# The first stage of a hybrid encoder layer: three row tiles with the contraction outside, shared modulation rows, and TensorE kept busy in waits

## The chip, the cores and the metric

The kernel runs on one core of one Trainium2 chip. A core has five engines, each with a queue of its own that runs in order: TensorE (PE, matmuls; its weight loads are PEld), VectorE (DVE), ScalarE (ACT), GpSimd (POOL) and SyncE (SP, which issues most transfers here). The metric is the time of one execution on the device in microseconds (us); lower is better.

## The reference

One layer of an encoder over x of 2048 rows and 1024 channels, in f32. What matters here is its beginning:

```
mod = silu(c) @ w_mod + b_mod                       # 6 x 1024 values
shift1, scale1, ... = split(mod, 6)
hmix = rms_norm(x, g_norm1) * (1.0 + scale1) + shift1
proj = hmix @ w_in                                  # 1024 x 2832
q_a, k_a, v_a, q_m, k_m, v_m, o_m, gates = split(proj)
```

Behind it come windowed attention and a chunked mLSTM in both directions, an output projection, and a SwiGLU feed-forward part, each with its modulation, and a last norm. These are not touched.

## The kernel before

The rows are worked in tiles of 128 (`tt`, 0 to 15), four of which make a block `n` (512 rows). The channels are worked in tiles of 128 as well (`k`, 0 to 7, `KT` = 8); `z` = 0 is the half with k from 0 to 3, `z` = 1 the half from 4 to 7. Products keep f32 accuracy by splitting each operand in a high and a low part; `mm3` (L56 to L58) issues three matmuls for one product: high by high, high by low, low by high.

The first stage makes, for every row tile, the columns of the projection that are needed in row order: 128 for the attention's values and 16 gates (with 128 of the mLSTM's values they make the 272 columns of `pa`), and the other 384 of the mLSTM's values (`pv`). `nat_mm` (L397) runs over k for `pa` and then for `pv`. The weights come in raw (`wnr`, `load_nat`, L330) and `split_nat` (L340) makes the high part `wnh` on ScalarE and the low part `wnl` on VectorE and GpSimd in turns (L342 to L347).

The moving-in of a block of x: `squares` (L163) sums the squares of its four row tiles on ScalarE (L168), `rsqrt` (L92) takes the root on VectorE in twelve small instructions, `scaled` (L171) multiplies (block 0 on ScalarE, L175; the others on VectorE, L177). `turned` (L179) turns one channel tile of the block by four transposes on TensorE (L183), and ScalarE applies scale and shift while reading it out of PSUM (`ntmp`, L184). `turned_split` (L186) splits the outcome in the high and low part of `hT` on VectorE (L190, L191). The scale `gs1` is (1 + scale1) x g_norm1.

Scale and shift are the modulation rows m = 1 and m = 0. Each half row (m, z) takes 1024 x 512 weights, loaded by `load_mod` (L195, four loads of 512 KB, L201) into eight slots, of which (1, 0) and (1, 1) share four and (0, 0) and (0, 1) the other four. `mod_sum` (L206) works one half row: VectorE multiplies the weights of a channel tile by its value of silu(c) and adds them up in `macc` (L213 the first, L215 the others). For (1, 0) and (0, 1) TensorE does the first four of the eight channel tiles instead (L220: one column of silu(c) against 512 columns of weights, in f32, so two records each) and adds the sum over the partitions of `macc` to them (L221); ScalarE copies the row (L223) and TensorE lays it out as four columns (L226). For the other two, TensorE lays out `macc` directly (L230). `mod_bias` (L237) adds b_mod on VectorE, `scales` (L328) makes gs1.

The order of this stage is written out by hand (L404 to L439). TensorE keeps the order of the program in the whole kernel. The other engines keep it up to `pre.close()` (L439); instructions from behind that line are put between those of the hand-ordered part by a scheduler that works from estimated times. The order on TensorE is: m = 1's and m = 0's columns for z = 0, the turns of channel tiles 0 to 3 of block 0, the projection of row tiles 0, 1 and 2 one after the other over k = 0 to 3, then the modulation for z = 1, the turns of channel tiles 4 to 7, and then the loop over n and i (L444), which finishes row tiles 0, 1 and 2 over k = 4 to 7 and goes on with row tile 3 and the other blocks. In it `EVERY` says after how many steps of `nat_mm` a channel tile of the next block is turned. A row tile's columns are read out of PSUM by ScalarE and VectorE (L478 to L482) and stored.

SP's queue loads, in this order: c, x of block 0, the weights of (1, 0) and (0, 0), the first half of `wnr`, (1, 1), the second half of `wnr`, (0, 1), x of blocks 1 and 2 (each tile 512 KB, L293), and the small rows. `columns_of` (L308) turns small rows (biases, gains, convolution weights) into columns; the second such turn (L452) stands ahead of row tile 4.

PSUM has eight banks, handed out by `bank` (L52) under the letters g, a, c (two each) and b, d (one each). A bank or an SBUF slot is handed on only when its last reader is done.

## Time and profile before

| | |
|---|---|
| median of 3 runs | 2271.92 us (2271.91 to 2275.42) |
| the profiled execution | 2273.35 us |
| its span, first to last instruction | 2271.6 us |
| mean granted TensorE clock | 0.996 |

A row of a timeline gives the start in us from the span's start, the duration, the engine, the line and the operation, out<-in by the program's names, their sizes, how many instructions are merged in the row, and in brackets how long the engine had been idle before it and what released it. A row of the windows gives a stretch of time, its length, the busy time of PE, PEld, DVE, ACT and POOL with the number of instructions that start in it, then the granted TensorE clock, the busy share of the DMA engines and their GB/s.

### The profile page before, as it was taken

Reading aid. Unit: us, or ns where it says so; the run is one execution under the profiler, and the core shown is the slowest. Engines: PE = TensorE matmul, PEld = TensorE weight load, DVE = VectorE, ACT = ScalarE, POOL = GpSimd, SP = SyncE. Lnnn points to the kernel's source line nnn. Section 1 sums busy time; section 2 is a strip of 40 time slices with the busy share of each in tenths; the row PEclk is TensorE's granted clock in tenths of the full one; section 3 lists DMA queues with packets and bytes.
Section 4 is the critical chain, followed back from the end, with each engine's and each line's share of the span. In section 5 each row is a group of like instructions: output and inputs, shape, how many; then the busy total and the mean of one; then the engine's idle time right before and its main releaser. Section 6 shows DMA issues by size and latency. Waiting matters only on the chain.

```text
span 2271.6 us, 32440 instructions
## 1 busy us (share of the span) xinstructions
PE 2222.6 (98%) x10822; PEld 1856.6 (82%) x10822; DVE 1618.5 (71%) x2931; ACT 1059.6 (47%) x2206; POOL 1065.6 (47%) x927
## 2 busy tenths in 40 slices
PE   6999999999999999999999999999999999999998
PEld 4997888888888878788888888788888888888886
DVE  6787577656788887786767786766767666785594
ACT  4533656544687746354445444433333333233352
POOL 1006635434334334536666665657565654692020
PEclk9999999999999999999999999999999999999999
DMA  8577755675766576764343454433333374542462
GB/s 321 171 245 220 236 168 168 186 239 173 214 186 180 172 244 209 258 239 152 109 145 114 149 181 162 158 98 111 98 112 98 112 251 148 168 152 94 142 219 93
DMA packets 352811, 391.28 MB, mean 172 GB/s; under 512 B 21260, under 2 KB 251004, under 8 KB 352644
## 3 DMA queue, kind: packets, MB, share of 16 engines
q1 hardware_dynamic: 352420, 389.18, 52.3%
q8 instruction: 85, 1.39, 0.3%
q14 instruction: 82, 0.67, 0.1%
q10 hardware_dynamic: 224, 0.04, 0.0%
HBM read 269.95 MB, written 119.19 MB: 171 GB/s over the span
## 4 chain that ended last, share of the span: by engine, by line
PE 55%; DMA 1%; DVE 1%; issue 1%; POOL 1%; ACT 0%; SPq 0%; POOLq 0%; ACTq 0%
PE fp L56 12%; PE fp L57 12%; PE fp L58 12%; PE fo L57 6%; PE fo L58 6%; PE fo L56 6%; PE ops L56 1%; PE ops L57 1%; PE ops L58 1%; DMA al<-a_d 0%; PE trn L183 0%; DMA T<-hop_d 0%; DMA a_d<-c 0%; DVE T L1417 0%; DMA w2n<-in_w_ffn_out_dram 0%
## 5 line engine op out<-in xcount | busy, mean ns | idle before, releaser
L498 PE MATMUL gps<-hT,whi 128*128 128x512 f32 x1088 | 395.4, 418 | 0.3 <-DVE cacc L513 0.3
L57 PE MATMUL fo<-w,ah 128*128 128x512 f32 x616 | 239.8, 389 | 0.7 <-DVE w L1726 0.7
L58 PE MATMUL fo<-w,al 128*128 128x512 f32 x616 | 239.9, 389 | 0.0
L56 PE MATMUL fo<-w,ah 128*128 128x512 f32 x616 | 239.7, 389 | 0.0
L498 PE MATMUL gps<-hT,wlo 128*128 128x512 f32 x544 | 226.0, 416 | 0.0
L498 PEld LDWEIGHTS gps<-hT,whi 128*128 128x128 f32 x1088 | 199.4, 190 | 24.3 <-DVE cacc L513 0.7
L56 PE MATMUL fp<-T,S 128*128 128x512 f32 x528 | 206.7, 391 | 0.2 <-ACT s L1613 0.2
L57 PE MATMUL fp<-T,S 128*128 128x512 f32 x528 | 205.7, 389 | 0.0
L58 PE MATMUL fp<-T,S 128*128 128x512 f32 x528 | 205.4, 389 | 0.0
L1717 DVE TENSOR_TENSOR al<-al,ah 128x1024 fp32r<-128x1024 f32 x77 | 116.4, 1516 | 107.7 <-ACT ah L1716 107.6
L1716 ACT ACTIVATE ah<-al 128x1024 fp32r<-128x1024 f32 x77 | 81.5, 1060 | 183.1 <-DMA al<-a_d 180.3
L1456 DVE TENSOR_TENSOR S<-sf,S 128x512 fp32r<-128x512 f32 x86 | 132.4, 1577 | 34.3 <-ACT S L1455 34.1
L1621 DVE SCALAR_TENSOR_TENSOR g<-t,g 128x512 f32<-128x512 f32 x44 | 46.4, 1055 | 131.8 <-ACT t L1620 131.8
L1456 DVE TENSOR_TENSOR A<-graw,A 128x512 fp32r<-128x512 f32 x86 | 132.1, 1556 | 11.5 <-ACT A L1455 11.5
L58 PE MATMUL fp<-B,A 128*128 128x512 f32 x352 | 136.9, 389 | 0.0
L56 PE MATMUL fp<-B,A 128*128 128x512 f32 x352 | 136.9, 389 | 0.0
L57 PE MATMUL fp<-B,A 128*128 128x512 f32 x352 | 136.9, 389 | 0.0
L57 PEld LDWEIGHTS fo<-w,ah 128*128 128x128 f32 x616 | 115.6, 188 | 25.1 <-DVE w L1726 1.1
L58 PEld LDWEIGHTS fo<-w,al 128*128 128x128 f32 x616 | 115.6, 188 | 24.5 <-DVE al L1717 0.3
L56 PEld LDWEIGHTS fo<-w,ah 128*128 128x128 f32 x616 | 115.6, 188 | 24.1
L798 POOL TENSOR_SCALAR ap<-ap,adn 128x384 f32<-128x384 f32 (+1 forms) x128 | 72.0, 582 | 126.7 <-PE atp L805 61.9
L1460 POOL TENSOR_TENSOR sf<-A,A22r 128x512 f32<-128x512 f32 x43 | 59.6, 1387 | 147.0 <-DMA A22r<-in_w_ffn_in_dram 131.9
(418 smaller groups left out, 6166.5 us busy)
## 6 DMA issues: line engine op xcount, KB each, us to landing
al<-a_d SPq DMA_DIRECT2D x77, 512.0 KB, 4.0
wmod<-in_w_mod_dram SPq DMA_DIRECT2D x48, 512.0 KB, 7.3
graw<-in_w_ffn_in_dram SPq DMA_DIRECT2D x43, 512.0 KB, 3.6
a_d<-ka SPq DMA_DIRECT2D x66, 256.0 KB, 4.6
bc<-bc_d SPq DMA_DIRECT2D x64, 256.0 KB, 3.7
hop_d<-n SPq DMA_DIRECT2D x56, 256.0 KB, 4.4
a_d<-u SPq DMA_DIRECT2D x55, 256.0 KB, 4.4
mqk<-qk_d SPq DMA_DIRECT2D x44, 256.0 KB, 3.9
```

The costliest lines, as they stand in the source:

```text
L56: pe.matmul(o, lh, rh, start=first, stop=False, skip_group_check=skip)
L57: pe.matmul(o, lh, rl, start=False, stop=False, skip_group_check=skip)
L58: pe.matmul(o, ll, rh, start=False, stop=last, skip_group_check=skip)
L498: pe.matmul(ps, w[i == 2][:, k, :], hT[n](i == 1, k), start=(k == 0 and i == 0), stop=(k == KT - 1 and i == 2))
L798: pool.tensor_scalar(self.p[g][:, :self.NK], self.p[g][:, :self.NK], dn[:, g:g + 1], 0.0, MUL, ADD)
L1456: dve.tensor_tensor(t[:, 1, :], f, t[:, 0, :].bitcast(F32), SUB)
L1460: pool.tensor_tensor(f1, a21, a22, ADD)
L1621: dve.scalar_tensor_tensor(g0, t0, 1.0, g0, ADD, MUL)
L1716: act.activation(ah, al.bitcast(F32), AF.Copy)
L1717: dve.tensor_tensor(al, al.bitcast(F32), ah.bitcast(F32), SUB)
```

## The change

Five things are changed, all in the first stage. (1) Row tiles 0, 1 and 2 are worked together, with k outside (`three`): as soon as a channel tile is split, the three row tiles use it. Channel tiles 0 to 2 are used before the second half's modulation, 3 in the middle of it, 4 to 6 behind it, and 7 in the loop. The weights' high and low parts are made one channel tile ahead (`nat_hi`, `nat_lo`), all low parts on VectorE. (2) The modulation's half rows become objects (`Mod`). TensorE's and VectorE's shares are interleaved; (0, 0) has two of its eight channel tiles on TensorE, (1, 1) none, the other two four. Row and sums of (0, 0) and (0, 1) are added as columns in PSUM, not as a row. The weights of (0, 1) are loaded ahead of the second half of `wnr`. (3) VectorE's sums of (1, 1) and (0, 1) follow each other without a break. (4) `steady` issues f32 matmuls of x by the identity into a bank that nobody reads, nine in all. (5) The second turn of small rows moves from ahead of row tile 4 to behind row tile 5. Besides, `scaled` gives two of the four row tiles of every block to ScalarE.

```diff
@@ -171,70 +171,83 @@
     def scaled(xt, r, on_act=False):
 
         for i in range(4):
-            if on_act:
+            if on_act or i % 2:
                 act.activation(xt[i], xt[i], AF.Copy, scale=r[:, i:i + 1])
             else:
                 dve.tensor_scalar(xt[i], xt[i], r[:, i:i + 1], None, MUL)
 
-    def turned(t, xt, k, tag, gs, shift):
...
+    def turns(xt, k, tag):
 
         ps = bank(tag, "trn")
         for i in range(4):
             pe.transpose(ps[:, i * P:(i + 1) * P], xt[i][:, k * P:(k + 1) * P], ident)
+        return ps
+
+    def turned(t, xt, k, tag, gs, shift):
+
+        act.activation(t, turns(xt, k, tag), AF.Identity, bias=shift[:, k:k + 1], scale=gs[:, k:k + 1])
+
+    def turned_split(pl, xt, k, gs, shift, dst, ps=None):
+
+        t = pl.tile([P, 512], F32, tag="ntmp", name="ntmp", bufs=2)
+        if ps is None:
+            ps = turns(xt, k, "bd"[k % 2])
         act.activation(t, ps, AF.Identity, bias=shift[:, k:k + 1], scale=gs[:, k:k + 1])
...
+    class Mod:
+
+
+        def __init__(self, m, z):
+            self.m, self.z, self.acc, self.ps, self.w = m, z, None, None, []
+            for k in range(0, KT, 2):
+                w = big(wm_slots[0], "wmod", (P, 2, 512), F32)
+                wm_slots.rotate(-1)
+                sp.dma_start(w, w_mod[k * P:(k + 2) * P, m * D + z * 512:m * D + (z + 1) * 512]
+                             .rearrange("(k p) c -> p k c", p=P))
+                self.w.append(w)
+
+        def sums(self, pl, ks):
+
+            for k in ks:
+                w = self.w[k // 2][:, k % 2, :]
+                if self.acc is None:
+                    self.acc = pl.tile([P, 512], F32, tag="macc", name="macc")
+                    dve.tensor_scalar(self.acc, w, sc_col[:, k:k + 1], None, MUL)
+                else:
+                    dve.scalar_tensor_tensor(self.acc, w, sc_col[:, k:k + 1], self.acc, MUL, ADD)
+
+        def rows(self, ks, tag, joined):
+
+            self.ps = bank(tag, "modrow")
+            for k in ks:
+                pe.matmul(self.ps[:1, :], sc_col[:, k:k + 1], self.w[k // 2][:, k % 2, :], start=k == ks[0],
+                          stop=k == ks[-1] and not joined)
+
+        def join(self):
+            pe.matmul(self.ps[:1, :], ones[:, 0:1], self.acc, start=False, stop=True)
+
+        def copy(self, pl):
+            self.row = pl.tile([1, 512], F32, tag="mrow", name="mrow", bufs=1)
+            act.activation(self.row, self.ps[:1, :], AF.Copy)
+
+        def columns(self, ps, row, first, last):
+
+            self.cs = ps
+            src, one = (self.row, ones[:1, 0:1]) if row else (self.acc, ones[:, 0:1])
             for k in range(4):
-                pe.matmul(ps[:, k:k + 1], row[:, k * P:(k + 1) * P], ones[:1, 0:1], start=True, stop=True)
-        else:
-            ps = bank("d", "modps")
-            for k in range(4):
-                pe.matmul(ps[:, k:k + 1], acc[:, k * P:(k + 1) * P], ones[:, 0:1], start=True, stop=True)
-        yield True
-        mod_bias(m, z, ps)
-        yield True
-
-    def mod_bias(m, z, ps):
-        o = O_BM + m * KT + 4 * z
-        dve.tensor_tensor(mod[:, m, 4 * z:4 * z + 4], ps[:, :4], cols[:, o:o + 4], ADD)
+                pe.matmul(ps[:, k:k + 1], src[:, k * P:(k + 1) * P], one, start=first and k == 0, stop=last, skip_group_check=True)
+
+        def bias(self):
+            m, zs = self.m, slice(4 * self.z, 4 * self.z + 4)
+            o = O_BM + m * KT + 4 * self.z
+            dve.tensor_tensor(mod[:, m, zs], self.cs[:, :4], cols[:, o:o + 4], ADD)
+            if m:
+                o = O_G1 + 4 * self.z
+                dve.scalar_tensor_tensor(gs1[:, zs], mod[:, 1, zs], 1.0, cols[:, o:o + 4], ADD, MUL)
...
-        wm = {(m, 0): load_mod(m, 0) for m in (1, 0)}
+        m10, m00 = Mod(1, 0), Mod(0, 0)
...
         def columns_of(z, o, n):
-            ps = bank("ad"[z], "colps")
+            ps = bank("ac"[z], "colps")
...
-        def split_nat(z, r):
-            ks = BD[z]
-            act.activation(wh[:, ks, :144], r[0], AF.Copy)
-            dve.tensor_tensor(wl[:, ks, :144], r[0], wh[:, ks, :144].bitcast(F32), SUB)
-            for i in range(4):
-                k, v = 4 * z + i, r[1 + i // 2][:, i % 2]
-                act.activation(wh[:, k, 144:], v, AF.Copy)
-                (pool, dve)[i % 2].tensor_tensor(wl[:, k, 144:], v, wh[:, k, 144:].bitcast(F32), SUB)
+        def nat_hi(z, r, i):
+            if i < 0:
+                act.activation(wh[:, BD[z], :144], r[0], AF.Copy)
+            else:
+                act.activation(wh[:, 4 * z + i, 144:], r[1 + i // 2][:, i % 2], AF.Copy)
+
+        def nat_lo(z, r, i):
+            w, o = (r[0], (BD[z], slice(0, 144))) if i < 0 else (r[1 + i // 2][:, i % 2], (4 * z + i, slice(144, None)))
+            dve.tensor_tensor(wl[:, o[0], o[1]], w, wh[:, o[0], o[1]].bitcast(F32), SUB)
...
         wn = [load_nat(0)]
-        wm[1, 1] = load_mod(1, 1)
+        m11, m01 = Mod(1, 1), Mod(0, 1)
         wn.append(load_nat(1))
-        wm[0, 1] = load_mod(0, 1)
...
-        ms = {(m, z): mod_sum(s1, m, z, wm[m, z], 4 if m == 1 - z else 0) for z in range(2) for m in (1, 0)}
-        ssq = squares(s1, xts[0])
+        x0, sh1 = xts[0], mod[:, 0, :]
+
+        def steady(ps, n):
+
+            for _ in range(n):
+                pe.matmul(ps, ident, x0[0][:, :512], start=True, stop=True)
+
+        idle = bank("a", "idle")
+        steady(idle, 6)
+        ssq = squares(s1, x0)
         r = rsqrt(s1, ssq, 4, D, "rs")
-        next(ms[1, 0])
-        scaled(xts[0], r, True)
-        next(ms[0, 0])
-        next(ms[1, 0])
-        next(ms[1, 0])
-        next(ms[0, 0])
-        next(ms[0, 0])
-        scales(0)
-        split_nat(0, wn[0])
+        m10.rows((0, 2, 4, 6), "g", True)
+        m10.sums(s1, (1, 3, 5, 7))
+        scaled(x0, r, True)
+        m10.join()
+        m10.copy(s1)
+        m00.rows((0, 2), "a", False)
+        m00.sums(s1, (1, 3, 4))
+        m10.columns(bank("c", "modps"), True, True, True)
+        m10.bias()
+        m00.copy(s1)
+        m00.sums(s1, (5, 6, 7))
+        trn = {k: turns(x0, k, "bd"[k]) for k in range(2)}
+        cs = bank("c", "modps")
+        m00.columns(cs, True, True, False)
+        nat_hi(0, wn[0], -1)
+        nat_hi(0, wn[0], 0)
+        nat_lo(0, wn[0], -1)
+        steady(idle, 1)
+        m00.columns(cs, False, False, True)
+        m00.bias()
+        nat_lo(0, wn[0], 0)
+        steady(idle, 1)
         ops = {i: (bank("gga"[i], "pa"), bank("acc"[i], "pv")) for i in range(3)}
+
+        def three(k, then=()):
+
+            for i in range(3):
+                deque(nat_mm(0, i, *ops[i], (k,)), 0)
+                if i == 0:
+                    for k_ in then:
+                        trn[k_] = turns(x0, k_, "bd"[k_ % 2])
+
         for k in range(4):
-            turned_split(s1, xts[0], k, gs1, mod[:, 0, :], hT[0])
-        for i in range(3):
-            deque(nat_mm(0, i, *ops[i], range(4)), 0)
-        next(ms[1, 1])
-        split_nat(1, wn[1])
-        next(ms[1, 1])
-        next(ms[1, 1])
-        next(ms[0, 1])
-        next(ms[0, 1])
-        next(ms[0, 1])
-        scales(1)
+            turned_split(s1, x0, k, gs1, sh1, hT[0], trn[k])
+            if k < 3:
+                nat_hi(0, wn[0], k + 1)
+                nat_lo(0, wn[0], k + 1)
+                three(k, (k + 2,) if k < 2 else ())
+        m11.sums(s1, range(KT))
+        m01.rows(range(4), "b", False)
+        m01.sums(s1, range(4, KT))
+        nat_hi(1, wn[1], -1)
+        m01.copy(s1)
+        for i in range(4):
+            nat_hi(1, wn[1], i)
+        cs = bank("d", "modps")
+        m11.columns(cs[:, :4], False, True, True)
+        nat_lo(1, wn[1], -1)
+        nat_lo(1, wn[1], 0)
+        m11.bias()
+        m01.columns(cs[:, 4:8], True, True, False)
+        three(3)
+        m01.columns(cs[:, 4:8], False, False, True)
+        m01.bias()
+        trn[4] = turns(x0, 4, "b")
+        steady(bank("d", "idle"), 1)
+        trn[5] = turns(x0, 5, "d")
         for k in range(4, KT):
-            turned_split(s1, xts[0], k, gs1, mod[:, 0, :], hT[0])
+            turned_split(s1, x0, k, gs1, sh1, hT[0], trn[k])
+            if k < 7:
+                nat_lo(1, wn[1], k - 3)
+                three(k, (k + 2,) if k < 6 else ())
         pre.close()
...
             if n == 1:
                 vecs = mod_row(2)
-                columns_of(1, N_A, N_B)
-                dve.tensor_scalar(cvw, cols[:, O_CW:O_CW + 24].rearrange("p (j k) -> p j k", j=3), 0.5, None, MUL)
-                dve.tensor_scalar(cvb, cols[:, O_CB:O_CB + KT], 0.5, None, MUL)
-                dve.tensor_scalar(gml, cols[:, O_GM:O_GM + HM], 0.5, None, MUL)
...
-                for j, _ in enumerate(nat_mm(n, i, pa, pv, range(4 if tt < 3 else 0, KT))):
+                for j, _ in enumerate(nat_mm(n, i, pa, pv, range(7 if tt < 3 else 0, KT))):
                     if ev and j % ev == ev - 1:
                         next(nrm, None)
+                if tt == 5:
+                    columns_of(1, N_A, N_B)
+                    dve.tensor_scalar(cvw, cols[:, O_CW:O_CW + 24].rearrange("p (j k) -> p j k", j=3), 0.5, None, MUL)
+                    dve.tensor_scalar(cvb, cols[:, O_CB:O_CB + KT], 0.5, None, MUL)
+                    dve.tensor_scalar(gml, cols[:, O_GM:O_GM + HM], 0.5, None, MUL)
```

31 lines of the change are left out of this document (removed).

## The prediction

> **What bounds the kernel now.** The page's first part and the windows of the whole span come first.
>
> ```profile
> PE 2222.6 (98%) x10822; PEld 1856.6 (82%) x10822; DVE 1618.5 (71%) x2931; ACT 1059.6 (47%) x2206; POOL 1065.6 (47%) x927
> 0.00:60.00 60.00, 41.83 (x189) 29.14 (x190) 38.30 (x86) 31.16 (x51) 6.98 (x14) 0.91 0.86 325
> 60.00:120.00 60.00, 59.08 (x414) 58.11 (x413) 47.53 (x117) 29.60 (x57) 0.84 (x8) 1.00 0.45 145
> ```
>
> TensorE sets the time: 98% busy, and 18.2 of its 49 idle us lie in the first 60. There the granted clock is also low (0.91, against 1.00). So whatever makes TensorE finish the first row tiles earlier moves everything behind it, because its later work is queued in program order and no later stage starts at a fixed time. The question is when tile 2 is finished; before, that is the start of tile 3.
>
> The windows by stage and the timeline of TensorE (start, duration, line, idle in brackets) show what the first stage waits for.
>
> ```profile
> 24.00:28.65 4.65, 4.28 (x20) 3.88 (x21) 3.73 (x7) 2.62 (x5) 2.08 (x2) 0.50 1.05 403
> 28.65:43.38 14.73, 14.10 (x75) 12.96 (x73) 12.82 (x18) 5.58 (x9) 3.22 (x3) 0.87 1.06 406
> 43.38:53.30 9.92, 8.54 (x44) 4.27 (x43) 4.12 (x10) 3.54 (x6) 0.00 (x0) 1.00 0.41 165
> ...
> 5.62 0.32 PE L310 MATMUL colps<-ident,rows 56*128 56x56 f32 x1 [2.92 <-DMA rows<-in_b_mod_dram]
> 11.65 5.38 PE L220 MATMUL modrow<-wmod,sc_col 128*1 128x512 f32 x8 [5.71 <-DMA wmod<-in_w_mod_dram]
> 18.77 1.05 PE L226 MATMUL modps<-ones_r,mrow 1*128 1x1 f32 x8 [0.68 <-ACT mrow L223]
> 22.99 1.86 PE L230 MATMUL modps<-ones_r,macc 128*128 128x1 f32 x8 [3.17 <-DVE macc L215]
> 28.65 0.50 PE L56 MATMUL pa<-wnh,hT 128*128 128x272 f32 x1
> 43.38 0.95 PE L230 MATMUL modps<-ones_r,macc 128*128 128x1 f32 x8
> 44.26 3.59 PE L220 MATMUL modrow<-wmod,sc_col 128*1 128x512 f32 x8
> 47.69 1.02 PE L221 MATMUL modrow<-macc,ones_r 128*1 128x512 f32 x2
> 50.69 1.10 PE L183 MATMUL trn<-ident,xt 128*128 128x128 f32 x8 [0.26 <-DVE mod L237]
> 59.18 0.29 PE L56 MATMUL pa<-wnh,hT 128*128 128x272 f32 x1
> 62.79 0.29 PE L56 MATMUL pa<-wnh,hT 128*128 128x272 f32 x1
> 66.39 0.29 PE L56 MATMUL pa<-wnh,hT 128*128 128x272 f32 x1
> ```
>
> The reader sees three losses. The first projection starts only at 28.65. It then runs to 43.38 (14.73 us) for three half tiles; a half tile at full clock takes 62.79 - 59.18 = 3.6 us, so 10.8 would do. And from 43.38 to 53.30 TensorE does no projection at all, because the second half's modulation is chained through it. The two L230 rows show the clock: the same eight records take 1.86 us at clock 0.50 and 0.95 at 1.00.
>
> **The change, part by part.** The first chain ends in the shift of channel tiles 0 to 3. The durations on the other engines are these.
>
> ```profile
> 13.72 4.27 ACT L175 ACTIVATE xt<-xt,rsy 128x1024 f32<-128x1024 f32 x4 [2.22 <-DVE rsy L106]
> 17.46 5.47 DVE L215 SCALAR_TENSOR_TENSOR macc<-wmod,sc_col,macc 128x512 f32<-128x512 f32 x7
> 18.13 0.59 ACT L223 ACTIVATE mrow<-modrow 1x512 f32<-1x512 f32 x1
> 22.87 2.38 ACT L346 ACTIVATE wnh<-wnr 128x512 fp32r<-128x512 f32 x4 [0.46 <-DMA wnr<-in_w_in_dram]
> 24.97 1.13 DVE L328 SCALAR_TENSOR_TENSOR gs<-mod,cols 128x4 f32<-128x4 f32 x1
> 26.20 1.45 ACT L184 ACTIVATE ntmp<-trn,mod,gs 128x512 f32<-128x512 f32 x2 [0.94 <-DVE gs L328]
> 40.53 1.29 DVE L347 TENSOR_TENSOR wnl<-wnr,wnh 128x512 fp32r<-128x512 f32 x2
> 50.55 0.15 DVE L328 SCALAR_TENSOR_TENSOR gs<-mod,cols 128x4 f32<-128x4 f32 x1
> 52.19 0.43 DVE L190 CAST hT<-ntmp 128x512 fp32r<-128x512 f32 x1 [1.49 <-ACT ntmp L184]
> 52.66 0.69 DVE L191 TENSOR_TENSOR hT<-ntmp,hT 128x512 fp32r<-128x512 f32 x1
> ```
>
> *Six steady matmuls.* An f32 matmul over 512 columns is two records; L220 has eight for four. Warm, one takes 3.59/8 = 0.45 us; at half speed (1.86 to 0.95 in L230) 0.88. The row from 11.65 adds up to 5.38 with four slow and four warm ones: the speed rises after some 3.6 us, though the clock's column has no record of it that early. Twelve records start behind L310 at 5.95. Rising in the same way they end at 5.95 + 3.6 + 8 x 0.45 = 13.1; if it never rises, at 16.5. Behind them in TensorE's queue stand m10's rows, and ScalarE's first `scaled`, which overwrites the tile that they read, would wait too. `scaled` starts at 13.72 anyway, so I take 0; the other end is 16.5 - 13.7 = 2.8 us on the whole first chain.
>
> *Shared modulation rows.* m10: two more rows on TensorE go (four remain, 3.6 us, to 16.7), joined by 17.7; the copy stands behind `scaled` at 18.0 as before, done 18.6. Then TensorE in order: m00's two rows 1.8 (19.5), m10's columns 1.05 (20.55), two turns 1.1 (21.65), m00's row columns 1.05 (22.7), one steady matmul 0.9 (23.6), m00's columns from the sums 0.95 (24.55). VectorE: a sum costs 5.47/7 = 0.78. m10's four end at 16.6, m00's first three by about 19.2 (they wait for the transfer), m10's bias waits for TensorE until 20.55 and holds back the last three sums, which end at 23.25; one low part follows. It is just in time. Shift ready at 24.75, against 24.97 + 1.13 before; the 1.13 was a clash with GpSimd's L347 (0.15 without it), and GpSimd has no low parts any more. ntmp 0.72 and the cast 0.43 put the first projection at 26.0, 2.65 earlier. The low parts that move to VectorE cost 0.65 each, one per channel tile, beside 2.7 us of matmul.
>
> *K outside.* A channel tile for three row tiles is 3 x 3.6/4 = 2.7 us. A turn of four transposes adds 0.44: the turns below repeat every 1.19 us around six L56 to L58 of 0.125 each.
>
> ```profile
> 67.15 0.60 PE L183 MATMUL trn<-ident,xt 128*128 128x128 f32 x4
> 68.34 0.60 PE L183 MATMUL trn<-ident,xt 128*128 128x128 f32 x4
> ```
>
> VectorE needs 1.06 for a split (cast to end of L191, less overlap) and 0.65 for a low part, 1.7 in all; ScalarE 0.72 + 0.6 (ntmp and L346). Both lie under 2.7. Only tile 0 waits 0.6 for the first L191. So k = 0, 1, 2 take 3.75, 3.14 and 2.7: TensorE is at 35.55. m01's rows need their weights. Those come from the loading order x0, m10, m00, wn0, m11, m01: five blocks of 2.10 MB and one of 1.34, 11.8 MB.
>
> ```profile
> 0.00:33.80 33.80, 17.82 (x60) 10.46 (x61) 20.21 (x46) 19.64 (x29) 5.28 (x13) 0.88 0.95 351
> 0.00:47.50 47.50, 31.52 (x132) 21.57 (x133) 30.83 (x60) 20.95 (x31) 6.98 (x14) 0.89 0.97 367
> 17.88 3.22 SPq L201 DMA_DIRECT2D wmod<-in_w_mod_dram  x4
> ```
>
> 351 GB/s x 33.8 us is 11.9 MB, so they are there. m01's four loads are moved ahead of wn1's and wait for m00's slots, the last one for the last m00 sum at 23.25. SP issues a load of this size every 3.22/4 = 0.8 us; m11's end at 21.1, so the fourth of m01 comes at about 23.6. SP does not stand still, nor do wn1 and the x loads queued behind it; the bound, if it did for a us, is covered by the 1.7 us between 33.8 and 35.5. x1 and x2 (4.2 MB) land by 47.5 in either order.
>
> *Second half.* m01's rows 3.6 (39.15), m11's columns 0.95 (40.1; VectorE's eight sums run 32.9 to 38.9), m01's row columns 1.05 (41.15; copy done 39.75), channel tile 3 2.7 (43.85), m01's last columns 0.95 (44.8; VectorE at 43.5), turn, steady, turn 1.8 (46.6). Then channel tiles 4 to 7: 3.65 + 3.14 + 2.7 + 2.7. **Tile 2 ends at 58.8, against 66.39: 7.6 us.**
>
> *Behind it.* The small rows' turn leaves a gap that TensorE had in front of tile 4; it moves behind tile 5, where their data has long landed and bank c is free:
>
> ```profile
> 78.29 0.26 PE L310 MATMUL colps<-ident,rows 48*128 48x48 f32 x1 [0.92 <-ACT ntmp L184]
> 66.39:78.48 12.09, 11.17 (x82) 10.60 (x81) 9.45 (x32) 9.42 (x20) 0.21 (x2) 1.00 0.40 114
> 56.70 0.16 DVE L99 TENSOR_SCALAR rsv<-ssq 128x4 f32<-128x4 f32 x1
> 58.95 2.74 DVE L177 TENSOR_SCALAR xt<-xt,rsy 128x1024 f32<-128x1024 f32 x4
> L479 DVE TENSOR_TENSOR vs<-pa,vs 128x128 fp32r<-128x128 f32 x3 | 0.9, 290 | 0.2 <-ACT vs L478 0.2
> ```
>
> That is +0.9. Against it stands crowding. Before, the roots (56.70 to 58.95, 2.25 us each) and scales of x1 and x2 lay under tiles 1 and 2. Now VectorE is free of the last split at 53.3, and tile 3's first turn comes at 59.6: 6.3 us for x1's root and its two scales (2.25 + 2 x 0.69 = 3.6; the other two scales are ScalarE's, 1.07 each) and three evictions (L479 0.29, and the gate's addition of about half that: some 1.3). x2's 3.6 fits to 1.4, and 2.2 goes into tile 3's stretch, where VectorE had 12.09 - 9.45 = 2.6 free. Between 0 and 2.5; I take 1.0, since it nearly fits. **Sum: 7.6 + 0.9 - 1.0 = 7.5 us.**
>
> The profiled execution took 2273.35 (span 2271.6 and 1.75 around it): 2265.85. It is 1.43 above the median, so the forecast for the median is 2271.92 - 7.5 = **2264.4 us**.
>
> **The rivals.**
>
> *Crowding (0.14).* Some of x3's work and all of x2's fall into tile 3: 3.7 is lost for 1.0. For it: VectorE and ScalarE were 78% busy there. Against it: x2 isn't needed before tile 4's ninth step. 7.6 + 0.9 - 3.7 = 4.8: 2267.1.
>
> *The clock falls anyway (0.18).* From 17.7 to 26 TensorE has turns, matmuls of one column and only 2.7 us of wide ones. If the clock halves at about 22.5, as in the stretch with clock 0.50, the columns and the steady matmul take 1.9 more, of which some 1.0 is late at the first projection, and 3.5 us of projections lose half, 1.8: 2.8 in all, 2267.2. For it: after L226 the clock was lost. Against it: the stretch 43.38:53.30 has 16 transposes and 16 small matmuls, and shows 1.00. [...]
>
> *Four squares ahead (0.11).* Only the first stage is ordered by hand; the squares of x1 and x2 are put between ScalarE's instructions.
>
> ```profile
> 39.20 1.06 ACT L168 ACTIVATE junk<-xt 128x1024 bf16<-128x1024 f32 x1 [5.24 <-DMA xt<-in_x_dram]
> 48.75 0.59 ACT L223 ACTIVATE mrow<-modrow 1x512 f32<-1x512 f32 x1 [8.39 <-PE modrow L221]
> ```
>
> One square stood ahead of the row's copy and waited 5.24 us for its transfer. One costs nothing here (39.15). If x1's four stand ahead, the last lands at about 42.2 (17.4 MB by 47.5 less four x2 tiles of 1.3 us), the copy comes at 43.5, 4.3 late: gain 3.2, 2268.7.
>
> *Eight ahead (0.07): slower.* The last of x2 lands at 47.5, its square ends at 48.75, the copy is 9.6 late; TensorE stands from 40.1 for 8.6 us, and loses the clock as it did after 3.17 idle us, 2.7 more. 12.3 - 7.5 = 4.8 slower: 2276.7. It decides from a copy later than 46.7, that is from the third x2 square on.
>
> **How the numbers follow.** 0.50 stays for the forecast. 0.2% is 4.5 us, about what a measurement tells from no change. Faster by more: nearly all of the forecast's (0.49), 0.09 of crowding and 0.12 of the clock, which lie at the edge: 0.70. Within: the rest of these and the four squares, 0.23. Slower: 0.07. The range: the order of the other engines behind the hand-ordered stage is made anew, and TensorE's 30.8 idle us behind 60 (49.0 - 18.2) may move a little by it; I allow 2.5. With that and no crowding the gain is 7.5 + 1.0 + 2.5 = 11 (2260.9; low end 2260.5); with four squares ahead and 1.8 of the same the other way it is 1.4 (2270.5). The likeliest alone holds 2262 to 2267.
>
> **What would show it.** First L56 at about 26.0; clock 1.00 from 16 to 59; m01's rows near 35.6; tile 3's first L56 at 58.8 (not 66.4); no gap ahead of tile 4, tile 3's stretch at most 12 us. Wrong would be: a window of 0.50 behind 22, VectorE's sums ending after 24.5, a row's copy on ScalarE behind a square, or a shift at 120 us that is lost again later.

## The result, and the profile after: slower by 0.17%

The changed kernel takes 2277.32 us in the median of 22 runs (2273.65 to 2282.59), the kernel before 2273.20 in 22 runs beside it (2270.03 to 2279.07). The ratio is 1.0017, with a 95% interval from 1.0011 to 1.0023: the change costs some 4 us, where 7.5 less were forecast. The profiled execution took 2275.14 us, near the low end of its runs, with a span of 2273.3; so the two traces stand only 1.7 us apart, and more than half of the loss isn't in this pair (the second profiled execution of the change, a0_again's below, has a span of 2276.8, 5.2 over before's). The median of before that the forecast started from, 2271.92 of three runs, was itself 1.3 low.

First the timeline of TensorE in the changed kernel (start, duration, line, records; in brackets the idle time ahead and who ended it). Lines have moved: the steady matmul is L427, rows L227, columns L242, the bias L247 and L250.

```profile
5.94 7.83 PE L427 MATMUL idle<-xt,ident 128*128 128x512 f32 x12
13.69 3.60 PE L227 MATMUL modrow<-wmod,sc_col 128*1 128x512 f32 x8
...
26.21 0.40 PE L56 MATMUL pa<-wnh,hT 128*128 128x272 f32 x1 [0.56 <-DVE hT L196]
...
35.88 3.59 PE L227 MATMUL modrow<-wmod,sc_col 128*1 128x512 f32 x8
39.54 1.02 PE L242 MATMUL modps<-ones_r,macc 128*128 128x1 f32 x8
43.64 1.83 PE L242 MATMUL modps<-ones_r,mrow 1*128 1x1 f32 x8 [3.08 <-DVE mod L247]
45.40 0.60 PE L56 MATMUL pa<-wnh,hT 128*128 128x272 f32 x1
...
49.54 0.95 PE L242 MATMUL modps<-ones_r,macc 128*128 128x1 f32 x8
...
52.34 0.37 PE L56 MATMUL pa<-wnh,hT 128*128 128x272 f32 x1
...
65.88 0.40 PE L56 MATMUL pa<-wnh,hT 128*128 128x272 f32 x1 [1.11 <-ACT va L538]
```

Down to the columns of m11 at 39.54 the stage runs as forecast, within 0.6 us at each point. Then comes a wait that the forecast doesn't have: m01's row columns start at 43.64 instead of 40.1. The bracket names L247, the addition of `m11.bias()` on VectorE. These are the timelines of VectorE and ScalarE there.

```profile
39.31 0.48 DVE L219 TENSOR_SCALAR macc<-wmod,sc_col 128x512 f32<-128x512 f32 x1
39.83 2.33 DVE L221 SCALAR_TENSOR_TENSOR macc<-wmod,sc_col,macc 128x512 f32<-128x512 f32 x3
42.07 1.35 DVE L358 TENSOR_TENSOR wnl<-wnr,wnh 128x576 fp32r<-128x576 f32 x2
43.34 0.15 DVE L247 TENSOR_TENSOR mod<-modps,cols 128x4 f32<-128x4 f32 x1
```

```profile
39.51 0.59 ACT L235 ACTIVATE mrow<-modrow 1x512 f32<-1x512 f32 x1 [2.25 <-PE modrow L227]
40.01 2.17 ACT L354 ACTIVATE wnh<-wnr 128x512 fp32r<-128x512 f32 x4
42.09 1.04 ACT L168 ACTIVATE junk<-xt 128x1024 bf16<-128x1024 f32 x1
```

ScalarE had copied m01's row by 40.1, so the data of the row columns were there. What was not free is their place: `m11.columns(cs[:, :4], ...)` and `m01.columns(cs[:, 4:8], ...)` share one PSUM tile, and `m11.bias()` reads it. The read stands on VectorE behind m01's four sums (to 42.1) and two low parts (to 43.4), and the write of m01 waits for it, although it goes to other columns. TensorE then loses its clock as well. The windows of the changed kernel (length, busy us of each engine, granted clock, DMA share, GB/s):

```profile
17.98:26.21 8.23, 7.67 (x41) 4.61 (x40) 5.88 (x12) 3.97 (x8) 0.00 (x0) 1.00 1.07 394
...
41.54:48.37 6.83, 4.73 (x19) 4.75 (x20) 2.11 (x5) 3.97 (x8) 0.00 (x0) 0.50 0.88 359
48.40:66.00 17.60, 16.23 (x108) 14.79 (x107) 12.47 (x42) 13.50 (x23) 0.00 (x0) 1.00 0.32 121
```

At 0.50 the row columns take 1.83 instead of 1.05 and channel tile 3 takes 4.14 (45.40 to 49.54) instead of 2.7. Tile 2 ends at 64.77 (65.88 less the wait of 1.11) instead of 58.8, and tile 3 starts at 65.88, half a us ahead of before's 66.39. That is nearly all of the forecast gain, gone within ten us.

Behind it, the same TensorE instruction stands in the two traces as follows (start in after less start in before): -1.5 us at tile 4 (no gap any more), -1.2 at 94.7 us, -0.9 at 161, -0.1 at 179, +0.1 at 800, -1.5 at 823.7, -0.3 at 847, +1.4 at 1016, +2.1 at 2014. Two stretches take most of the time back (0.8 us more go between 1400 and 1460 and were not followed). One is the modulation rows of `mod_row`, from 95 to 180 us. The waits of TensorE from 100 to 190 us (total, count, longest), first of the kernel before, then of the changed one:

```profile
PE modrow L381 <- ACT macch L141: 1.3, 2, 0.7
```

```profile
PE modrow L392 <- ACT macch L141: 2.2, 3, 1.7
```

There TensorE waits for the high part (`macch`) that ScalarE makes of a sum of VectorE's; what it comes earlier, it waits longer. In the longest of these waits, 1.7 us up to 179.05, VectorE's sum was done at 177.4, but ScalarE had a weight tile to split first (L264, 177.42 to 178.48), for which it had itself waited on a load. The other stretch is near 845 us, the first output projection. The timeline of the kernel before, and the window behind it:

```profile
838.63 0.36 SPq L1061 DMA_DIRECT2D ma<-mxa_d  x1
843.35 1.16 ACT L1075 ACTIVATE msq<-ma 128x512 f32<-128x512 f32 x2 [1.15 <-DMA ma<-mxa_d]
847.05 0.38 PE L1125 MATMUL aps<-ones_r,msq 128*128 128x1 f32 x2 [0.88 <-POOL msq L1077]
```

```profile
847.00:851.00 4.00, 3.95 (x18) 3.28 (x19) 3.18 (x16) 0.72 (x1) 1.24 (x1) 1.00 0.60 192
```

The same two of the changed kernel, and a row of its DMA queues for 834 to 843 us (packets, MB, share of 16 engines):

```profile
836.97 0.36 SPq L1118 DMA_DIRECT2D ma<-mxa_d  x1
843.10 1.15 ACT L1132 ACTIVATE msq<-ma 128x512 f32<-128x512 f32 x2 [2.56 <-DMA ma<-mxa_d]
845.13 0.38 PE L1182 MATMUL aps<-ones_r,msq 128*128 128x1 f32 x2 [0.73 <-POOL msq L1134]
846.80 0.38 PE L1182 MATMUL aps<-ones_r,msq 128*128 128x1 f32 x2 [1.28 <-POOL msq L1134]
```

```profile
847.00:851.00 4.00, 4.00 (x12) 3.19 (x12) 2.96 (x16) 0.99 (x1) 0.97 (x1) 0.57 0.14 51
```

```profile
q8 instruction: 1, 0.02, 0.7%
```

From the issue of the load of `ma` to its square it is 4.72 us before and 6.13 after. TensorE waits twice instead of once, and the clock falls behind it (0.57 over these 4 us). In the clock's record of both traces the stretches behind the first change are whole multiples of 3.41 us (two such steps at 0.50 from 41.54 to 48.37 above, one from 847.08 to 850.50; the last stretch alone is cut off by the end), called clock windows here. In the kernel before, the eight records of L230 take 1.86 us at 0.50 and 0.95 at 1.00; worked out from that, a TensorE that is busy at 0.50 through one window loses some 1.7 us, half of it (an estimate). Behind 180 us both kernels have the same instructions in the same order on every engine, so the cause must be something that the order doesn't show. The neighbours in SP's queue are issued at the same distances behind the load in both (x_d 0.6, xr 2.7, mm 3.3 us). What differs is the last row. A transfer of the kind "instruction" falls into the load (16,384 bytes by its record; 0.7% of 16 engines over 9 us is 1.0 us on one of them). In before that window holds none: its transfers fall at 817 and 849 us. The page counts 86 of this queue after and 85 before. The change gives TensorE 36 more matmul records and 36 more weight loads (10858 against 10822), 72 instructions; before's trace has 21,937 of TensorE's instructions to 85 transfers, 258 to each (from the first transfer to the last 255.5 on average, in both traces; the runs below take 256). By these counts 72 more move every later transfer by 28% of its interval ahead, and the two of 817 and 849 us stand at 807 and 840 in the changed kernel's trace. What that costs is what the runs below try.

The kernel before seems to have such a loss itself, 25 us earlier, where one of its transfers (817.28 to 818.30) comes just ahead of the square of an earlier load of `ma`:

```profile
819.65 1.15 ACT L1075 ACTIVATE msq<-ma 128x512 f32<-128x512 f32 x2 [1.99 <-DMA ma<-mxa_d]
823.73 0.38 PE L1125 MATMUL aps<-ones_r,msq 128*128 128x1 f32 x2 [1.27 <-POOL msq L1077]
```

In the changed kernel this square has 1.23 us of idle time ahead of it and TensorE doesn't wait at its matmul; that is where -1.5 at 823.7 comes from. That this wait is the transfer's doing was not tried. From 800 to 1016 us the change therefore loses 1.3 us against before, less than the 2.9 that one counts from 823.7.

### The profile page after: what moved, and what is told of

Its sections match the earlier page's. It is cut to its first block, busy times and chain, and to the rows that moved or that the text cites. A ratio compares the mean times of both kernels' runs of the same rounds, so it can differ in the third digit from the quotient of the medians.

```text
span 2273.3 us, 32509 instructions
## 1 busy us (share of the span) xinstructions
PE 2231.4 (98%) x10858; PEld 1860.8 (82%) x10858; DVE 1607.9 (71%) x2927; ACT 1066.7 (47%) x2213; POOL 1059.9 (47%) x923
## 4 chain that ended last, share of the span: by engine, by line
PE 54%; DVE 3%; DMA 1%; issue 1%; ACT 0%; SPq 0%; DVEq 0%; ACTq 0%
PE fp L57 12%; PE fp L56 12%; PE fp L58 12%; PE fo L58 5%; PE fo L57 5%; PE fo L56 5%; PE ops L56 1%; PE ops L57 1%; PE ops L58 1%; DVE ra L1917 1%; DVE w L1783 0%; DMA al<-a_d 0%; DVE al L1774 0%; DVE T L1474 0%; PE trn L183 0%
## 5 line engine op out<-in xcount | busy, mean ns | idle before, releaser
L1513 DVE TENSOR_TENSOR S<-sf,S 128x512 fp32r<-128x512 f32 x86 | 127.0, 1514 | 32.9 <-ACT S L1512 32.8
```

What stands on the lines that cost most here:

```text
L1513: dve.tensor_tensor(t[:, 1, :], f, t[:, 0, :].bitcast(F32), SUB)
```

## The experiments

Each was timed over five rounds beside the kernel before on the same chip. Ratios are to that kernel, with their 95% intervals. The first four runs shared one chip and the later ones ran on three others, so ratios are the safer comparison between the groups; 0.001 is 2.3 us. A difference between two traces is the start of the same TensorE instruction in the one less that in the other.

**The changed kernel once more.** It gives the scatter, and the partner for the others.

> The changed kernel once more, beside the others on one chip. Every theory: ratio to the kernel before between 1.001 and 1.0025, row tile 3 starts near 65.9 us. If the 1.4 us that its trace lost between 80 and 180 us, and the second fall of the clock near 847 us, belong to the kernel, they are here again; if they belong to one execution, the stall at the last modulation row or the fall is elsewhere or gone.

2278.36 us, ratio 1.0015 [1.0006, 1.0024]. The wait of the row columns and the late square are there again (2.31 us of idle time ahead of the square). The clock fell at 1446 us too, which it did not in the first trace, and the span is 2276.8: one execution differs from another by several us in which of the fixed stalls costs the clock.

**The bias moved behind channel tile 3.** The order on VectorE stays as it is; but in the program the bias, which reads the shared tile, now stands behind the row columns, so that their write need not wait for it.

```diff
         nat_lo(1, wn[1], 0)
-        m11.bias()
         m01.columns(cs[:, 4:8], True, True, False)
         three(3)
+        m11.bias()
         m01.columns(cs[:, 4:8], False, False, True)
```

> One line moved: m11's bias on VectorE behind channel tile 3 in the program. Theory A (m01's row columns wait on TensorE for that bias, because both halves' columns lie in one PSUM tile and the bias reads it; the 3.1 us of waiting also cost the clock): no wait ahead of the row columns, channel tile 3 at full clock, row tile 3 starts 5 to 6 us earlier, near 60. If nothing behind it takes that back, the ratio to the kernel before is 0.999 to 1.000 (about 5.5 us under the changed kernel). Theory B (the stage behind, its modulation rows and ScalarE's and VectorE's order, decides when the stage ends): row tile 3 is earlier, but by 180 us the start of the last modulation row is less than 2 us earlier than in the changed kernel, and the ratio stays at 1.001 to 1.002.

2273.83 us, ratio 0.9995 [0.9986, 1.0003], 4.5 us under a0_again. Its TensorE timeline and windows:

```profile
40.00 1.02 PE L242 MATMUL modps<-ones_r,macc 128*128 128x1 f32 x8
40.95 1.05 PE L242 MATMUL modps<-ones_r,mrow 1*128 1x1 f32 x8
41.93 0.40 PE L56 MATMUL pa<-wnh,hT 128*128 128x272 f32 x1
...
61.40 0.29 PE L56 MATMUL pa<-wnh,hT 128*128 128x272 f32 x1
```

```profile
39.15:42.56 3.41, 3.35 (x22) 2.56 (x21) 3.30 (x6) 2.58 (x5) 0.00 (x0) 1.00 1.03 419
42.56:45.98 3.42, 3.42 (x15) 3.42 (x14) 1.56 (x5) 0.09 (x1) 0.00 (x0) 0.50 1.02 419
```

The wait is gone and tile 3 starts at 61.40, 5.0 us ahead of before. The clock still falls, for one window, though TensorE was at work for 3.35 of the 3.41 us ahead; 2.0 of them (40.00 to 42.00) are matmuls of one column. So the wait's share is shown, and with it that the bias made the row columns wait, as theory A says. That the shared tile is what ties them is read from the code: no run gave the two results tiles of their own. Theory B's numbers did not come (at 179 us the kernel is 2.2 us ahead of the changed one's first trace, where B allowed less than 2), but its mechanism is there: of 6.2 us at tile 4 (against before) 4.5 are left at 104 and 2.3 at 179, and the wait for `macch` grows to 3.2 us. In this trace the late square and the fall at 845 are there too (2.30 us of idle time ahead of the square), and 0.5 us is left at the end.

**The scales as before** (the blocks x1 to x3 wholly on VectorE; block 0 is ScalarE's in all these kernels, so "every block" in the list of changes means these three).

```diff
-            if on_act or i % 2:
+            if on_act:
```

> The changed kernel with the scaling of x1, x2 and x3 on VectorE alone, as before. If giving half of it to ScalarE is what costs (ScalarE's queue ahead of the reads of PSUM and of the modulation rows), the ratio falls by 0.001 or more against the changed kernel, and the 1.6 us wait near 179 us is gone. If it helps as I assumed, tile 3 and tile 4 start up to 1.4 us later and the ratio is the same or up to 0.001 higher.

2278.10 us, ratio 1.0014 [1.0005, 1.0022]: nothing to tell from a0_again. The split of the scales is not where the time went.

**The small rows alone, in the kernel before** (their turn behind tile 5 and in bank c, as in the diff).

> The kernel before with one part of the change alone: the small rows' turn moved behind row tile 5. My term: the gap of 0.92 us ahead of row tile 4 is gone and tile 4 starts 0.9 to 1.2 us earlier; ratio 0.9995, which a run can hardly tell from 1. Rival: the time is lost again behind tile 5, or the new order of the other engines costs more than it gives: ratio above 1.0005.

2272.33 us, ratio 0.9993 [0.9985, 1.0002], 1.9 us under before, which the interval can't tell from nothing. In the trace tile 4 starts 2.9 us earlier, of which 1.2 stood already at 55 us, ahead of the edit; 1.3 are left at 189.

**72 instructions more, in the kernel before.** Tiny matmuls are put where TensorE waits for `w_mod` anyway.

```diff
         columns_of(0, 0, N_A)
+        pd = bank("d", "pad")
+        for _ in range(18):
+            pe.matmul(pd[:1, :1], ones[:1, 0:1], ones[:1, 0:1], start=True, stop=True)
```

> The kernel before with 18 float32 matmuls of 1x1 added on TensorE behind the columns of the small rows (5.9 to 11.6 us, where TensorE waited for w_mod), nothing else. A float32 matmul gives two matmul and two weight-load records, so TensorE's program gets 72 instructions longer, as in the change. Theory C (the change lost its second half because 72 more instructions shift where the 16 KB instruction transfers fall: in the changed kernels one falls at 837 to 841 us, into the load of ma from mxa_d, whose square then takes 5.5 to 6.1 us instead of 4.6 to 4.7, and the clock falls again at 844 to 850): the milestones up to 800 us stay within 0.5 us of before, an instruction transfer falls between 837 and 842, the square msq takes 5.4 to 6.2 us, the clock falls at 844 to 850, and the time is 1 to 3 us over before, ratio 1.0005 to 1.0013. Rival D (the later loss belongs to the changed start's arrival times, not to the instruction count): msq stays near 4.6 us, no fall at 844 to 850, ratio 0.9995 to 1.0003.

2277.39 us, ratio 1.0017 [1.0008, 1.0026], more than theory C's 1.0005 to 1.0013: 18 matmuls that take 1.03 us inside a wait of 5.7 cost 3.4 us. The square and the queue's row, 834 to 843 us:

```profile
844.25 1.15 ACT L1078 ACTIVATE msq<-ma 128x512 f32<-128x512 f32 x2 [2.65 <-DMA ma<-mxa_d]
```

```profile
q8 instruction: 1, 0.02, 0.9%
```

The late square has come to the kernel before. Up to 800 us the trace strays from before's by -0.7 (59 to 120 us) to +1.4 (189), more than the 0.5 expected; it is late by 0.5 at 800, 0.9 at 847, 0.6 at 1016 and 1.2 at 2014. The clock did not fall at 844 to 850 in this execution, against the expectation, but did at 1440. So the transfer moved as theory C has it, but between 800 and 1016 this trace loses only 0.1 us by it, and all milestones together account for a third of the 3.4 us; the rest lies in executions without a trace (the profiled one, 2274.54, is the fastest of its 11).

**The changed kernel, bias moved, and 184 instructions more** (30 of the tiny matmuls ahead of `columns_of(0, ...)`, 16 behind), so that 72 + 184 = 256 is one whole transfer by the 255.5 of the two traces.

> The changed kernel with m11.bias() behind three(3), and 46 float32 matmuls of 1x1 added on TensorE (30 ahead of the columns of the small rows, 16 behind, both where TensorE waits), 184 instructions, so that together with the change's 72 the program is 256 instructions (one 16 KB transfer) longer than before. Theory C: the instruction transfers fall at the same work as in the kernel before (817 and 849), none in the load of ma; msq near 4.6 us, no fall at 844 to 850, and the time is 2 to 3.5 us under e1_bias_later (2273.8), 2270 to 2272, ratio to before 0.998 to 0.9991. Rival D: the same as e1_bias_later within 1 us, ratio 0.9990 to 1.0000. Should the 46 matmuls cost time at the start (they may delay the columns of the small rows by up to 2 us, which nothing waits for before the biases at 23), the tile milestones to 100 us show it.

2270.58 us, ratio 0.9982 [0.9973, 0.9992]: faster than both kernels, 3.4 us under before. The square and the windows:

```profile
836.26 1.15 ACT L1138 ACTIVATE msq<-ma 128x512 f32<-128x512 f32 x2 [0.67 <-DMA ma<-mxa_d]
```

```profile
15.00:60.00 45.00, 43.90 (x253) 33.37 (x252) 33.19 (x69) 27.45 (x46) 0.00 (x0) 1.00 0.90 342
820.00:850.00 30.00, 29.26 (x138) 23.74 (x137) 25.38 (x49) 13.48 (x22) 13.55 (x11) 1.00 0.43 141
```

The square is on time and the clock stays at 1.00 in both stretches, the first one too, where e1_bias_later lost it with the same instructions. Against before, tile 4 starts 7.8 us earlier, 6.2 are left at 104, 4.5 to 5 from 189 to 588, 7 at 847, 5.3 at the end. Against e1_bias_later's trace it is 1.6 us ahead at tile 4, where it kept the clock's window, 2.6 at 800 and 5.2 at 1016: so about half of what separates the two there was gained ahead of the first output projection.

**The same 184 instructions in the changed kernel as it is.**

> The changed kernel as it is with the same 46 matmuls of 1x1 (184 instructions), so that its program is 256 instructions longer than before. Theory C: msq near 4.6 us, no clock fall at 844 to 850, and 2 to 3.5 us under a0_again (2278.4): 2274.5 to 2276.5, ratio 0.9998 to 1.0010. Rival D: as a0_again, ratio 1.0010 to 1.0022.

2275.46 us, ratio 1.0008 [1.0000, 1.0017], 2.9 under a0_again (0.0007 by the ratios); 0.78 us of idle time ahead of the square, and no fall at 844 to 850. Against the first trace of the change it stays within 0.8 us up to 160 us, and is 2.4 us ahead at 800 and 3.6 by 1018.

**The steady matmuls made tiny**, with the instruction count kept. There are nine of them (six, then three single ones), not the eight that the expectation counts.

```diff
-                pe.matmul(ps, ident, x0[0][:, :512], start=True, stop=True)
+                pe.matmul(ps[:1, :1], ones[:1, 0:1], ones[:1, 0:1], start=True, stop=True)
```

> The changed kernel with each of its 8 steady matmuls (128x512, there to keep TensorE busy while it waits) made a matmul of 1x1, so that the instruction count stays as in a0_again and TensorE idles. The prediction's reading of the clock (0.50 in windows that are mostly idle, 1.00 from 16 us because of the steady matmuls): the clock stays at 0.50 to past 15 us and the rows of m10 take about 6 to 7 us instead of 3.60, the first L56 at 28 to 30 instead of 26.2, and the tiles behind are 2 to 4 us late at 65 us; absorbed by half at 180 us, ratio 1.0015 to 1.003. Rival (the clock does not depend on them; a matmul of a waiting stage is waste): first L56 within 0.5 us of 26.2, ratio as a0_again 1.0010 to 1.0022, and part of the rows earlier since nothing stands ahead of them.

2280.25 us, ratio 1.0026 [1.0017, 1.0035], 1.9 over a0_again, with intervals that overlap. TensorE's timeline and one window:

```profile
11.67 6.38 PE L227 MATMUL modrow<-wmod,sc_col 128*1 128x512 f32 x8 [5.37 <-DMA wmod<-in_w_mod_dram]
17.89 1.02 PE L231 MATMUL modrow<-macc,ones_r 128*1 128x512 f32 x2
...
27.69 0.59 PE L56 MATMUL pa<-wnh,hT 128*128 128x272 f32 x1 [1.42 <-DVE hT L196]
```

```profile
24.14:30.97 6.83, 5.26 (x22) 4.82 (x23) 4.89 (x10) 2.54 (x5) 0.00 (x0) 0.50 1.05 408
```

m10's rows take 6.38 instead of 3.60, but start 2 us earlier, so they end only 0.8 later (17.89 against 17.12); the first projection comes 1.5 us later, at half clock. The direction is the one expected, and the first projection comes a little sooner than the 28 to 30 that were expected. At tile 3 this trace is 1.3 us behind a0_again's and 2.1 behind the first one's: in these traces that is what the steady matmuls are worth there.

**Whole transfers and others, in the kernel before and in e1.** 64 tiny matmuls (256 instructions) and 46 (184) in before, split over the two places as in e3_bias_later_pe46; 23 (92, with the change's own 164) in e1_bias_later, all in the first.

> The kernel before with 64 matmuls of 1x1 (256 instructions, one whole 16 KB transfer), 30 ahead of the columns of the small rows and 34 behind them. Theory C: the transfers fall at the same work as in before (one ahead of the load of ma, one behind its square), the wait ahead of msq is 0.7 to 1.2 us, and the time is that of before: ratio 0.9995 to 1.0005, although 46 more matmuls were added than in b2_before_pe18. Rival E (each added matmul or the work at the start costs the time): ratio at or over that of b2_before_pe18, 1.0017 or more.

> The kernel before with 46 of these matmuls (184 instructions). By the places of the transfers in before (817 and 849 us) the second falls at about 826 us, ahead of the load of ma (834 to 843). Theory C: wait ahead of msq 0.7 to 1.2 us, ratio 0.9990 to 1.0005, unless the shifted transfers meet another load elsewhere, which the milestones would show. Rival E: ratio between 1.0012 and 1.004.

> The changed kernel with m11.bias() behind three(3) and 23 of these matmuls ahead of the columns of the small rows: 92 instructions, with the change's 72 together 164. Theory C: the transfer falls at about 828 us, ahead of the load of ma; wait ahead of msq 0.6 to 1.2 us, and the time within 1 us of e3_bias_later_pe46 (2270.6), ratio 0.9977 to 0.9987. Rival F (only the alignment of the kernel before is good, by whatever it meets elsewhere): ratio 0.999 to 1.0005 as e1_bias_later.

b3: 2274.91 us, ratio 1.0009 [1.0000, 1.0017]. b4: 2276.81, 1.0019 [1.0010, 1.0028]. e5: 2271.40, 0.9991 [0.9982, 1.0000]. All three lie above what theory C gave: b3 between it and rival E, b4 in rival E's range, e5 in rival F's (though within 1 us of e3 by the median). The square is on time in all three (0.79, 0.75 and 0.78 us of idle time ahead of it), so that part of theory C holds wherever it was tried. The times are not explained by it. In b3 and b4 a transfer now falls into the loads at the very start, where before has none ahead of 39 us. VectorE's first sums there (b3, the row of its queue from 8 to 16 us, then b4):

```profile
15.27 0.49 DVE L213 TENSOR_SCALAR macc<-wmod,sc_col 128x512 f32<-128x512 f32 x1 [1.00 <-DMA wmod<-in_w_mod_dram]
```

```profile
q8 instruction: 1, 0.02, 0.7%
```

```profile
17.97 0.49 DVE L213 TENSOR_SCALAR macc<-wmod,sc_col 128x512 f32<-128x512 f32 x1 [0.86 <-DMA wmod<-in_w_mod_dram]
```

In b3 the sums start 1.15 us later than in before (14.12 there), in b4 a sum waits 0.86 that waited for nothing there, and m00's columns are 1.2 and 1.1 us late. That fits the same mechanism in another place; but e3 and a1 have a transfer there too (at 10.8 and 11.3 us), and their first projection is only 0.4 us behind the changed kernel's first trace. Of the further 3.0 (b3) and 1.7 us (b4) that are lost up to 198 us, the clock's record places a part: both have a window at 0.50 at 57 to 62 us where before has none, and b4 another at 183. Up to 62 us b3 spends one window more at 0.50 than before (13.65 us in all against 10.24). Why the windows fall so is open, and rival E (added matmuls at the start cost time) is not excluded for them.

**The same 184 instructions at 820 us**, in the changed kernel, ahead of its first product with `mS`, so that nothing ahead of it differs.

```diff
+            for _ in range(46 if pr is first_ and u == 2 else 0):
+                pe.matmul(b5[:1, :1], ones[:1, 0:1], ones[:1, 0:1], start=True, stop=True)
             for k in range(4):
```

> The changed kernel with the 46 matmuls of 1x1 (184 instructions) put not at the start but into the first output projection, ahead of its third product (the first mS), where TensorE waits 1.79 us at 819.5 us in the trace of the change. Everything ahead of 819 us is then the changed kernel's, its transfers too; only those behind shift. Theory C: the transfer of 840 us falls ahead of 834 or behind 845, the wait ahead of msq is 0.6 to 1.2 us instead of 2.3 to 2.6, no clock fall at 844 to 850, the milestones up to 819 as in the change (tile 3, 94, 161, 179 within 0.5 us), those behind 850 are 2 to 3 us under a0_again's, ratio 0.9998 to 1.0008. Rival D: msq and the fall as in the change, ratio 1.0012 to 1.0022.

2274.95 us, ratio 1.0008 [0.9999, 1.0017], 3.4 under a0_again. Its timelines and window:

```profile
838.51 0.36 SPq L1118 DMA_DIRECT2D ma<-mxa_d  x1
843.06 1.15 ACT L1132 ACTIVATE msq<-ma 128x512 f32<-128x512 f32 x2 [0.98 <-DMA ma<-mxa_d]
846.77 0.38 PE L1182 MATMUL aps<-ones_r,msq 128*128 128x1 f32 x2 [0.70 <-POOL msq L1134]
```

```profile
847.00:851.00 4.00, 4.00 (x19) 3.29 (x19) 3.47 (x17) 1.02 (x1) 0.95 (x1) 1.00 0.53 173
```

Against the trace of a0_again it is within 0.5 us up to 823 (0.1 behind there), 1.5 us ahead at 848, and 3.3 ahead at 1019: 1.5 from the square that is no longer late, and the 1.7 of the clock window that is no longer lost. The transfers lie at 825 and 849. This is the plainest of the runs, since 46 useless matmuls make a kernel faster. By the times alone the two intervals (1.0006 to 1.0024 and 0.9999 to 1.0017) overlap; the trace places the gain. Taken together, the two padded runs stand 1.5 and 0.9 us over before by the medians, the two of the change as it is 4.1 and 4.2.

## Why the prediction was wrong

**Right, with its numbers.** The first projection at 26.21 (26.0 forecast), m01's rows at 35.88 (35.55), m11's columns at 39.54 (39.15), and 1.00 in the window from 17.98 to 26.21, where the clock's rival put the fall. The 0.9 us ahead of tile 4 came as 1.0 (-0.5 at tile 3, -1.5 at tile 4). Crowding was taken as 1.0: the wait of 1.11 us ahead of tile 3 is such a one, for an eviction (L538) that came late behind VectorE's scales of x2 (up to 65.2); e1_bias_later has none. Both rivals with squares of x1 and x2 ahead of the row's copy fell: the copy ran at 39.51, the first square at 42.09. That the one with eight squares gave 2276.7, close to the result, is luck: the copy it would have held up was on time (and its sum adds 9.6 us where it has TensorE stand for 8.6). One of the prediction's own signs of being wrong did come, a shift at 120 us (-1.1) that is lost later (-0.1 at 179).

**The step that failed** is "m01's row columns 1.05 (41.15; copy done 39.75), ... (VectorE at 43.5)". It lists what the row columns read and counts VectorE's 43.5 as slack against 44.8. It does not ask who still reads the tile that they write. The bias that VectorE runs at 43.34 reads `cs`, so the forecast's own number was the start of the next TensorE instruction. Cost: 3.08 us of waiting, 0.8 + 1.4 for row columns and channel tile 3 at half clock, together 5.3; removed alone in e1_bias_later, tile 3 comes 5.2 us earlier than in a0_again and the median falls by 4.5.

**The clock's rival** was put in the wrong place. The clock fell at 41 to 45 us in seven of the nine traces with the changed first stage: behind the wait, and in e1_bias_later without it, behind the one-column matmuls. In e3_bias_later_pe46 and e5_bias_later_pe23 it did not fall. The same instructions can lose the window or keep it: e1 had 2.0 us of one-column matmuls in one window and lost the next, e3 had 1.7 and e5 1.9 and kept it. The lost window of e1_bias_later runs from 42.56 to 45.98; the two of the change's first trace (41.54 to 48.37) don't lie on the same steps of 3.41 us.

**"No later stage starts at a fixed time"** was the assumption that carried 7.5 us undiminished to the end. It is partly wrong: at `mod_row` TensorE waits for sums that go through VectorE and ScalarE. From tile 4 to 179 us e1_bias_later loses 3.9 of 6.2 us, 3.0 of them from 95 us on, where `mod_row` is; e3_bias_later_pe46 loses 2.4 of 7.8, 1.6 of them there.

**What no part of the prediction had** is the loss behind 800 us. It counted the steady and extra matmuls by their duration and not as instructions. Where the 72 shift an instruction transfer into the load of `ma`, its square comes late: shown by a2_after_pe46_at_820, and by the square's wait, which is 1.9 to 2.9 us in each of the six traces with a transfer in the load (the change's two, e1_bias_later, e2_scale_vector, s1_no_steady and b2_before_pe18) and 0.7 to 1.2 in the eight with the transfer elsewhere. What that costs differs. A clock window at 844 to 850 is lost in five of the six and in none of the eight; but twelve of the fourteen traces, before's too, lose one at 816 to 828, and the two that don't (e2_scale_vector, s1_no_steady) are among the five. From 800 to 1016 us the six end up 0.1 to 1.8 us later against before's trace, the eight between 2.4 earlier and 0.5 later.

**The account.** From 2278.4 (a0_again), the bias moved takes 4.5 off, and the padding 3.3 more (e3 under e1; 0.0013 by the ratios): 2270.6, 3.4 under before. Not all of the 3.3 belongs to the first output projection: of the 4.7 us that the two traces differ by at the end, 2.6 stood already at 800 us. What is then still missing to 7.5 is mostly what e3's trace loses between tile 4 (7.8) and 198 us (5.0). Open remain the full size of the transfers' share (1.2 of the 3.4 us of b2_before_pe18 are placed in its trace, and e5, with the square on time, gains only 0.0004 on e1) and why b3 and b4 lose clock windows between 30 and 200 us.

## What to carry to other kernels

For each instruction that is moved ahead, list not only what it reads but who still reads the tile that it writes; here a PSUM tile shared by two small results held TensorE up for 3.08 us behind VectorE's queue, although they lie in different columns (that the tile is the tie is read from the code). A gain at the start is worth at the end what the next stage that waits for another engine lets through (of the 6.2 us of e1_bias_later at tile 4, 2.3 were left at 179 us), so look for that stage before the gain is summed up. And where two kernels differ by a few us far behind the change with the same order of work, compare the instruction transfers: here 72 instructions more put one into a load that is on the path (2.65 us of idle time ahead of its square in b2_before_pe18, 1.15 in before), and 184 of padding took it out again (0.98 in a2_after_pe46_at_820, 2.31 in a0_again). Padding moves the other later transfers too, though (in b3_before_pe64 one falls into the first loads, and VectorE's sums there start 1.15 us later), so it has to be tried.

## What the runs showed of the hardware

- An instruction transfer of 16,384 bytes, about 1 us on one of 16 DMA engines (1.01 in the changed kernel's trace, at 840 us), delayed a load of 512 KB that it met by about 1.4 us (issue of `ma` to its square: 6.13 against 4.72 us; 5.49 to 6.46 in the six traces with such a meeting, 4.24 to 4.72 in the eight without). There was one to 255.5 of TensorE's instructions on average, from the first transfer to the last, in the traces of both kernels.
- 46 matmuls that compute nothing made the changed kernel some 2 to 3 us faster (ratios 1.0008 and 1.0008 against 1.0015 and 1.0017; medians 2274.95 and 2275.46 against 2278.36 and 2277.32), and 18 made the kernel before 3.4 us slower.
- A window with TensorE busy for 3.35 of 3.41 us, but 2.0 of it on matmuls of one column, was followed by one at clock 0.50 (e1_bias_later, 39.15 to 45.98). With 1.9 us of them none followed (e5_bias_later_pe23, 37.93 to 41.34). That these matmuls weigh less than wide ones is a reading of the first, and was not tried alone.
